# Attention stages ahead of weight splits, and transposes later in TensorE's queue

## The chip, the cores and the metric

The kernel runs on one core of one Trainium2 chip. The metric is the device time of one execution in microseconds. The kernel was run three times: median 1540.57, from 1539.96 to 1541.12. One more execution was taken with the hardware profiler; all rows below come from it.

## The reference

Two blocks run one after the other on a sequence of 256 tokens of width 1024, in float32, each with its own two layers of weights (DEPTH = 2).

The first block's layer is a hybrid mixer, a cross attention and a gated feed-forward, each followed by a layer norm of a scaled residual sum:

```
mix = hybrid_mixer(h, ...)                    # RG-LRU branch and sliding-window attention, gated, projected
h = layer_norm(DEEPNORM_ALPHA * h + mix, ln1_g[l], ln1_b[l])
h = layer_norm(DEEPNORM_ALPHA * h + cross_attention(h, mem, ...), ln2_g[l], ln2_b[l])
h = layer_norm(DEEPNORM_ALPHA * h + swiglu(h, ffn_wi[l], ffn_wo[l]), ln3_g[l], ln3_b[l])
```

The sliding-window attention has 16 query heads and 2 key heads of width 64, rotary positions on the first 16 columns of a head, a window of 128 keys and a sink in the softmax. The second block's layer is differential attention (4 heads, each the difference of two softmaxes, with a relative bias) beside a Hyena branch (three short convolutions and two long convolutions through the Fourier transform), gated, projected and added to the input after an RMS norm:

```
h = rms_norm(x, pre_norm[l], NORM_EPS)
w = p[:, :, 0] - lam * p[:, :, 1]             # differential attention's weights
z = fft_long_conv(hv, filt[:, 0], flt_bias[l, 0]) * hx1
z = fft_long_conv(z, filt[:, 1], flt_bias[l, 1]) * hx2
x = x + rms_norm(m @ w_out[l], post_norm[l], NORM_EPS)
```

## The kernel before, in words

Every large matrix product is made of three matmuls: each operand is split into a high part of reduced precision (fp32r) and the rest, and high x high, high x low and low x high are summed in PSUM. Weights come from memory in chunks of 1 MB (three raw buffers, tag raw). `split_one` (from line 213) splits a chunk in two halves: ScalarE writes the high part wh (L229), VectorE the rest wl (L231), into four pairs of buffers, so that splits can run up to four halves ahead of the matmuls. `run_stream` goes through the chunks in order: before each half it lets due stages run (`pump`), issues the half's matmuls, and then the split of the half that is four further on. A half is 24 matmuls of 256 columns (`fm`, weights stationary) or 12 of 512 columns (`tm`, activations stationary), and `pump` is called once more in its middle.

Everything that is no chunk is written as a generator (a stage list) that is kept in a list with a due time: `ln_co` transposes a normed block of 128 tokens, `swa_co` rotates queries and keys, transposes them (kt, qt) and spawns two `swa_run` (one a key head), which make scores (sc), a softmax, transposes of the probabilities (pt) and the product with the values (y); `cross_co` does cross attention; `diff_co` does differential attention for one block of tokens (scores ds, transposes dw, product o); `hyena_co` the long convolutions (dft, c). Each `yield` gives the time until the next stage is due. The planner's clock `self.t` counts TensorE work alone: n/2.4 ns for a matmul of n columns (four times that for float32), 107 for a transpose. So the due times in the table `L` set how much TensorE work stands ahead of a stage in TensorE's queue, and TensorE (and the DMA queue of SP) run in just that written order (`MAN`).

ScalarE, VectorE and GpSimd are not in `MAN`: their order is made by the scheduler, which takes instructions by their place in the written program. `advance` runs a stage inside `high_priority(offset=co.pri)`, with `pri` from the table `PRI` by the generator's name: its instructions count as if written that many places earlier. Cross attention has had 60 there, the filters' transforms -60.

In a norm, `ln_evac` makes block 0 of the tokens first (L568, L571 write t), then block 1; `ln_co` yields `ln_0` (500), transposes block 0, yields `ln01` to `ln12` less `ln_0`, and transposes block 1 (tiles tx; ScalarE and VectorE split them, L350 and L351). Behind the last norm of the first block's cross attention no chunk stands, and the planner fills with filter pieces (fh). `rope` (5000) is the due time between the rotation on VectorE and the transposes of rotated keys (kd) and queries. PSUM has two pools of four tiles: one for `fm` products, one for all stages and `tm`.

Of the kernel before, what the change touches and what calls it, by code (L numbers as in the profile page):

```python
# [40 lines left out]
NSLOT = 29  # L41
NTMP = 8
NKEEP = 5
PRI = {'filter_dft': -60, 'cross_co': 60, 'filter_end': 30, 'rnn_co': 30, 'mlp_co': 60}

L = dict(
    vec=6000, flt=12000, fh=1200, fe=18000, prep=15000, mlp=7500, sc=11000, rnn=7000, rnn2=11700,
    pt=3000, tx=0, spec=6000, sp0=3000, sp1=5000, sp2=5000, sp3=5000, ds=9000, dn=8960, do=5500,
    z=12000, cn=1000, cp=2000, ln_0=500, ln01=3500, ln02=5500, ln03=6000, ln11=5000, ln12=4000, pre0=5100,
    pre1=5000, rope=5000, sw0=1120, sw_end=1500, sw1=1000, sw2=1500, cv0=800, cv1=1050, rnn3=1800,  # L50
    rnn_end=3000, cx0=1500, cx1=1000, cx2=800, cx_end=1500, ml=7200, fm=3000, fe0=4000, eo0=6000,
    eo1=12000, eo2=8000, fd=6000, di0=1500, dw=850, di_end=1500, c30=770, c31=1300, hy0=1300,
    hy1=2000, hy2=500, hy3=1600, hy_end=2000, pre_n=3000, pre_n1=2300, prep2=30000, mem=10200)
# [50 lines left out]
class Net:  # L104
# [26 lines left out]
    def spawn(self, gen, bg=False):  # L131
        co = Co(gen, self.t, PRI.get(gen.__name__, 0))
        (self.bg if bg else self.chains).append(co)
        return co
# [1645 lines left out]
```

## Time and profile before

| what | value |
|---|---|
| median of 3 runs | 1540.57 us |
| the profiled execution | 1539.61 us |
| its span, first to last instruction | 1537.7 us |
| TensorE busy (PE) | 1500.0 us, 98% |
| weight loads (PEld) | 1387.4 us, 90% |
| VectorE (DVE) | 1095.2 us, 71% |
| ScalarE (ACT) | 862.1 us, 56% |
| GpSimd (POOL) | 83.7 us, 5% |
| mean granted TensorE clock | 0.992 |

Matmuls are pipelined: one of 256 columns is shown with some 283 ns, but the next starts 120 ns behind it. So a gap in TensorE's queue is read from the starts, or from the wait that the timeline puts in brackets behind a row.

### The profile page before, as it was taken

To read this page: it belongs to the slowest core of one execution; us is meant where nothing else is said; L and a number is where in the kernel's file an instruction comes from. 1 tells how busy PE (TensorE), PEld (TensorE's weight loads), DVE (VectorE), ACT (ScalarE), POOL (GpSimd) and SP (SyncE) were. 2 spreads that over 40 slices of the span, in tenths; PEclk is the share of its full clock that TensorE was granted. 3 is DMA by queue.
4 is the path that set the end of the run, shared out by engine and by line. 5 is a ranking of instruction groups with operands and counts; after the bars stand their busy time and mean duration, and the time that the engine had idled before them with its cause. 6 is when DMAs were issued, how large, how long until landed. Compare 5 with 4: busy or idle time off the path is not lost. (4 is left out here: it accounts for less than half of the span.)

```text
span 1537.7 us, 25746 instructions
## 1 busy us (share of the span) xinstructions
PE 1500.0 (98%) x10588; PEld 1387.4 (90%) x10588; DVE 1095.2 (71%) x1590; ACT 862.1 (56%) x1338; POOL 83.7 (5%) x152
## 2 busy tenths in 40 slices
PE   8999999999999999999999999999999999999997
PEld 6889999989999989899989798999798998898996
DVE  5876767668665477858676776555897987797865
ACT  5789444545444445797445556644545755555742
POOL 4001000000000000001010010000000010000000
PEclk9999999999999999999999999999999999999998
DMA  8435655445545545436555476565355356354542
GB/s 284 139 111 165 219 182 175 170 160 196 188 165 191 191 165 165 138 119 224 192 190 194 151 245 195 166 240 191 98 160 178 118 166 216 112 170 137 162 157 80
DMA packets 202982, 263.93 MB, mean 172 GB/s; under 512 B 5491, under 2 KB 163413, under 8 KB 202864
## 3 DMA queue, kind: packets, MB, share of 16 engines
q1 hardware_dynamic: 197232, 246.43, 48.5%
q0 software_dynamic: 5632, 15.86, 3.6%
q8 instruction: 83, 1.36, 0.4%
q14 instruction: 35, 0.29, 0.1%
HBM read 261.21 MB, written 2.11 MB: 171 GB/s over the span
## 5 line engine op out<-in xcount | busy, mean ns | idle before, releaser
L231 DVE TENSOR_TENSOR wl<-raw,wh 128x1024 fp32r<-128x1024 f32 x464 | 567.1, 1226 | 294.6 <-ACT wh L229 292.6
L229 ACT ACTIVATE wh<-raw 128x1024 fp32r<-128x1024 f32 (+1 forms) x465 | 490.2, 1057 | 443.2 <-PE fm L361 247.7
L361 PE MATMUL fm<-n2h,wh 128*128 128x256 f32 x640 | 176.6, 286 | 1.2 <-ACT n2h L350 1.2
L361 PE MATMUL fm<-n2l,wh 128*128 128x256 f32 x640 | 174.7, 283 | 0.0
L361 PE MATMUL fm<-n2h,wl 128*128 128x256 f32 x640 | 174.5, 283 | 0.0
L361 PE MATMUL fm<-h2h,wh 128*128 128x256 f32 x704 | 171.4, 284 | 0.0
L361 PE MATMUL fm<-h2h,wl 128*128 128x256 f32 x704 | 170.8, 283 | 0.0
L361 PE MATMUL fm<-h2l,wh 128*128 128x256 f32 x704 | 170.7, 283 | 0.0
L361 PEld LDWEIGHTS fm<-h2h,wh 128*128 128x128 f32 x704 | 124.0, 192 | 3.6 <-issue 1.9
L361 PEld LDWEIGHTS fm<-n2h,wh 128*128 128x128 f32 x640 | 119.9, 192 | 3.3 <-ACT n2h L350 1.7
L361 PEld LDWEIGHTS fm<-h2h,wl 128*128 128x128 f32 x704 | 122.7, 192 | 0.1
L361 PEld LDWEIGHTS fm<-h2l,wh 128*128 128x128 f32 x704 | 122.7, 192 | 0.0
L361 PEld LDWEIGHTS fm<-n2l,wh 128*128 128x128 f32 x640 | 119.8, 192 | 0.4 <-DVE n2l L351 0.4
L361 PEld LDWEIGHTS fm<-n2h,wl 128*128 128x128 f32 x640 | 119.8, 192 | 0.2
L361 PE MATMUL fm<-h3h,wh 128*128 128x256 f32 x256 | 71.2, 288 | 0.0
L361 PE MATMUL fm<-xTh,wh 128*128 128x256 f32 x256 | 70.9, 287 | 0.0
L361 PE MATMUL fm<-h3h,wl 128*128 128x256 f32 x256 | 70.1, 284 | 0.0
L361 PE MATMUL fm<-h3l,wh 128*128 128x256 f32 x256 | 70.0, 284 | 0.0
L361 PE MATMUL fm<-xTh,wl 128*128 128x256 f32 x256 | 69.8, 283 | 0.0
L361 PE MATMUL fm<-xTl,wh 128*128 128x256 f32 x256 | 69.8, 283 | 0.0
L361 PE MATMUL ff<-wh,ah 128*128 128x512 f32 x176 | 68.9, 392 | 0.0
L361 PE MATMUL ff<-wl,ah 128*128 128x512 f32 x176 | 68.7, 390 | 0.0
(433 smaller groups left out, 3650.1 us busy)
## 6 DMA issues: line engine op xcount, KB each, us to landing
raw<-in_w_in_dram SPq DMA_DIRECT2D x89, 1024.0 KB, 5.2
raw<-in_ffn_wi_dram SPq DMA_DIRECT2D x44, 1024.0 KB, 5.0
raw<-in_ffn_wo_dram SPq DMA_DIRECT2D x22, 1024.0 KB, 4.8
raw<-in_w_out_dram SPq DMA_DIRECT2D x16, 1024.0 KB, 5.0
raw<-in_ckv_w_dram SPq DMA_DIRECT2D x16, 1024.0 KB, 5.4
raw<-in_w_br_attn_dram SPq DMA_DIRECT2D x8, 1024.0 KB, 5.0
raw<-in_w_br_rnn_dram SPq DMA_DIRECT2D x8, 1024.0 KB, 5.0
raw<-in_cq_w_dram SPq DMA_DIRECT2D x8, 1024.0 KB, 4.9
```

The source lines that it names most:

```text
L229: hi_ins = self.nc.scalar.activation(hi[:, i:i + q], s[:, i:i + q], AF.Copy)
L231: lo_ins = self.nc.vector.tensor_tensor(lo, s, hi.bitcast(F32), op=ALU.subtract)
L361: self.nc.tensor.matmul(out, lhsT=l, rhs=r, start=start, stop=stop)
```

## The change

Two entries are added to `PRI`: the stages of `swa_run` and of `diff_co` now count as written 60 places earlier. In `L`, `ln_0` goes from 500 to 2200 and `rope` from 5000 to 6400. No instruction is added or taken away.

```diff
-PRI = {'filter_dft': -60, 'cross_co': 60, 'filter_end': 30, 'rnn_co': 30, 'mlp_co': 60}
+PRI = {'filter_dft': -60, 'cross_co': 60, 'filter_end': 30, 'rnn_co': 30, 'mlp_co': 60,
+       'swa_run': 60, 'diff_co': 60}
 
 L = dict(
...
-    z=12000, cn=1000, cp=2000, ln_0=500, ln01=3500, ln02=5500, ln03=6000, ln11=5000, ln12=4000, pre0=5100,
-    pre1=5000, rope=5000, sw0=1120, sw_end=1500, sw1=1000, sw2=1500, cv0=800, cv1=1050, rnn3=1800,
+    z=12000, cn=1000, cp=2000, ln_0=2200, ln01=3500, ln02=5500, ln03=6000, ln11=5000, ln12=4000, pre0=5100,
+    pre1=5000, rope=6400, sw0=1120, sw_end=1500, sw1=1000, sw2=1500, cv0=800, cv1=1050, rnn3=1800,
```

## Rows read from the trace of the kernel before

**Rows 1.** The page: busy time by engine, granted clock in 40 slices, ScalarE's splits.
```profile
PE 1500.0 (98%) x10588; PEld 1387.4 (90%) x10588; DVE 1095.2 (71%) x1590; ACT 862.1 (56%) x1338; POOL 83.7 (5%) x152
...
PEclk9999999999999999999999999999999999999998
...
L229 ACT ACTIVATE wh<-raw 128x1024 fp32r<-128x1024 f32 (+1 forms) x465 | 490.2, 1057 | 443.2 <-PE fm L361 247.7
```

**Rows 2.** TensorE's waits: who waited for whom, us in total, times, longest.
```profile
PE tx L373 <- DVE t L571: 6.0, 4, 3.0
...
PE pt L373 <- ACT scs L669: 1.9, 1, 1.9
...
PE kt L373 <- DVE kd L610: 1.2, 1, 1.2
...
PE ds L361 <- DVE dsc L1432: 0.9, 2, 0.4
PE c L361 <- ACT wT L1464: 0.7, 2, 0.4
```

**Rows 3.** The chain that ended last: start, us, engine and line, count.
```profile
1135.17 2.87 PE fm L361 x24
```

**Rows 4.** TensorE's timeline, layer 0: start, us, instruction, count [idle before, releaser].
```profile
50.58 0.27 PE L373 MATMUL kt<-ident,kd 128*128 128x128 f32 x1
52.06 0.55 PE L373 MATMUL kt<-ident,kd 128*128 128x128 f32 x3 [1.20 <-DVE kd L610]
```

**Rows 5.** TensorE's timeline, sliding-window attention of layer 1.
```profile
626.83 1.13 PE L361 MATMUL sc<-kv,qT 64*128 64x256 f32 x8
...
642.43 2.17 PE L373 MATMUL pt<-ident,scs 128*128 128x128 f32 x8 [1.90 <-ACT scs L669]
```

**Rows 6.** VectorE's timeline in the same stretch.
```profile
636.85 1.28 DVE L658 SCALAR_TENSOR_TENSOR scs<-sc,mask 128x512 f32<-128x512 f32 x2
...
639.24 1.22 DVE L231 TENSOR_TENSOR wl<-raw,wh 128x1024 fp32r<-128x1024 f32 x1
...
640.44 1.22 DVE L231 TENSOR_TENSOR wl<-raw,wh 128x1024 fp32r<-128x1024 f32 x1
```

**Rows 7.** A window behind it: busy us (count) by engine, granted clock, DMA share, GB/s.
```profile
642.40:646.00 3.60, 3.57 (x16) 2.96 (x17) 0.38 (x3) 3.60 (x11) 0.00 (x0) 0.53 0.77 265
```

**Rows 8.** TensorE's timeline, differential attention of the second block's layer 0.
```profile
1217.44 1.13 PE L361 MATMUL ds<-qk,qk 64*128 64x256 f32 x6 [0.44 <-DVE dsc L1432]
1218.93 0.50 PE L361 MATMUL c<-Yh,dft 128*128 128x512 f32 x1 [0.36 <-ACT wT L1464]
```

**Rows 9.** VectorE's timeline in the same stretch.
```profile
1215.51 1.27 DVE L1378 TENSOR_TENSOR t<-AB 128x512 f32<-128x512 f32 x2
1216.71 0.67 DVE L1432 SCALAR_TENSOR_TENSOR dsc<-ds,bias 128x512 f32<-128x512 f32 x1
```

**Rows 10.** TensorE's timeline, norms behind feed-forward (layer 0) and cross attention (layer 1).
```profile
556.39 1.32 PE L373 MATMUL tx<-ident,t 128*128 128x128 f32 x8 [1.40 <-DVE t L571]
...
564.75 1.03 PE L373 MATMUL tx<-ident,t 128*128 128x128 f32 x8
...
884.72 1.93 PE L373 MATMUL tx<-ident,t 128*128 128x128 f32 x8 [3.04 <-DVE t L571]
```

**Rows 11.** VectorE's timeline in the same two stretches.
```profile
561.83 1.41 DVE L571 SCALAR_TENSOR_TENSOR t<-t,rs,gb 128x512 f32<-128x512 f32 x2
...
881.28 0.67 DVE L351 TENSOR_TENSOR h2l<-tx,h2h 128x512 fp32r<-128x512 f32 x1
```

**Rows 12.** VectorE's timeline in cross attention of layer 0.
```profile
292.85 1.22 DVE L231 TENSOR_TENSOR wl<-raw,wh 128x1024 fp32r<-128x1024 f32 x1
293.98 0.16 DVE L930 TENSOR_SCALAR cst<-cst 128x2 f32<-128x2 f32 x1
```

**Rows 13.** ScalarE's timeline at the gates of layer 1.
```profile
669.51 1.28 ACT L752 ACT_TABLE_LOAD   x1
```

**Rows 14.** A window over the gates of layer 1, columns as in rows 7.
```profile
664.00:690.00 26.00, 26.00 (x211) 24.04 (x210) 14.56 (x20) 25.17 (x57) 0.88 (x1) 1.00 0.51 163
```

## The prediction

> **What bounds the kernel now.** I read the page's first parts, then the waits of TensorE alone, then the timelines where one of its waits touches an attention or a norm. TensorE is busy for 98% of the span at full granted clock [rows 1]; no matmul is added or removed, so the change can only alter the gaps in TensorE's queue. Its whole queue order is written by the planner; ScalarE and VectorE get theirs from the scheduler. The gaps that the edited lines can reach are few [rows 2]: the norms' transposes 6.0 us in 4 waits, the probabilities' transposes 1.9 in one, the rotated keys' 1.2 in one, differential attention 0.9 and 0.7 in two each: 10.7 us of idle time in all. That, and what a lowered clock costs after a long gap, is the ceiling. The reader should see in the PE timelines that each gap names a VectorE or ScalarE instruction, and in the VectorE timelines what stood ahead of that instruction.
>
> The planner's clock decides places. A matmul of 256 columns is 256/2.4 = 106.7 ns on it, and it looks for due stages every 12 matmuls, 1280 ns. On the chip 24 matmuls take 2.87 us [rows 3], so one such step is 1.44 us of cover.
>
> **Rotated keys (rope 5000 to 6400).** In layer 0 the first kt transpose runs at 50.58, the second at 52.06 [rows 4]: 1.48 apart, where the three from there on take 0.55 together, so some 1.35 is lost to kd. 5000 falls due at the fourth step (5120). 6400 is five steps exactly, and the planner sums in floating point: starting from the planner's time at which the stage is spawned, 29666.000000000036, my sum at the fifth step is 36066.0 against a due time of 36066.00000000004, a hair early, so I expect the sixth step: 24 matmuls later. Either way (1.44 or 2.87) it is covered. Value: 1.4, bounds 1.2 to 1.5. Layer 1 has no gap here, so there the delay gains nothing; its whole chain of scores and transposes moves 2.9 later, and nothing asks for it before the output projections, 16 halves of 24 matmuls (46 us) after the gates. No DMA is issued by the moved transposes; SP's queue keeps its order.
>
> **Sliding-window stages ahead by 60.** The gap is in layer 1: the pt transposes wait 1.90 for exponentials [rows 5]. Their scores had left TensorE at 626.83 + 1.13 = 627.96, yet VectorE first touches them at 636.85, 8.9 later, and inside the chain two weight splits of 1.2 stand between the maxima and the negated maxima [rows 6]. VectorE was working off convolutions and splits in that time. Sixty places are about two and a half halves of 24 matmuls (7.2 us) of age, so the mask and maximum should go roughly 5 earlier even if the fills remain. Only the 1.90 is needed. After the gap the granted clock is 0.53 over 3.60 us [rows 7], a loss of 0.47 x 3.60 = 1.7. The Trainium skill, page "TensorE: Matmul & The Clock Gate", Part 1, says that the slow level is the default and that activity releases it; the trace agrees with 0.53 right behind this gap. By that rule a removed gap returns its 1.7 too, and a gap that is only halved may return nothing of it. Both ends: 0 (the fills decide, below) and 3.6; I take 3.3, because the chain moves by more than twice what is missing, less 0.3 for transposes that now meet the last of four exponentials.
>
> What pays is the splits. A split may start when its buffer is free, three halves (3 x 2.87 = 8.6) ahead of use, and takes 1.06 [rows 1] + 1.2; about 6.3 is in hand. One stage of scores is some 3 us of VectorE, and only splits younger than sixty instructions are overtaken, those needed last. I cost it at nothing; if a split already 4 us late were overtaken by a whole stage, TensorE would wait some 1 us, and that is in the range.
>
> **Differential attention ahead by 60.** In each layer of the second block the last scores wait for PSUM that L1432 has yet to read (0.44), then c waits for wT (0.36) [rows 8]; with the waits of both layers 1.6. L1432 runs at 1216.71, behind two L1378 of the Hyena chain [rows 9]. Going first it closes the gap, but then Hyena's Y pieces slip by up to three operations of 0.67 (2.0), and they feed the very c matmuls that come next; they finish about 2 before use now. What is late next is therefore c on Yl. Bounds: 1.6 gained, 1.5 lost; I take 0.8 gained, since c also starts on the older half of Y.
>
> **Norm transposes (ln_0 500 to 2200).** Block 0 of the tokens is due at the second step instead of the first. Block 1's due time is counted from there, so its step stays (worked through: fourth, fifth and fifth step for ln01, ln02, ln11, as before), but for ln03: before, 2136 + 5500 = 7636 misses the fifth look at 7256; now 3416 + 3800 = 7216 makes it. So at the end of layer 0's feed-forward block 0, which waited 1.40 [rows 10], gets 1.44 of cover, while block 1 moves from 564.75 to about 561.7; its data leave L571 at 561.83 + 0.7 = 562.5 [rows 11], a new wait of about 0.9. Net 0.5, bounds -0.2 and 1.4. At the end of layer 1's cross attention no weight chunk covers: two more filter pieces go ahead of block 0, and block 1 waits 3.04 for its data [rows 10]. There two h2l operations of block 0, 0.67 and as much again, stand between block 1's statistics and its normalization [rows 11]; later transposes make them unready, and the chain ends up to 1.3 earlier. I take 0.9, bounds 0 and 2.5 (with the clock given back). The first norm of layer 0 has the same form with one such operation, 0 to 0.6; I take 0.
>
> **Sum.** 1.4 + 3.3 + 0.8 + 0.5 + 0.9 = 6.9. The profiled execution took 1539.61 (span 1537.7 and 1.9 around it), 0.96 below the median 1540.57. 1539.6 - 6.9 = 1532.7, and 1533.7 on the scale of the median.
>
> **Rivals.**
> A, the priority does nothing where it matters. A scheduler that takes whatever is ready puts a split into the gap after each dependent operation. For it: cross attention has had its 60 all along, and still a split stands between its maximum and the scaled maximum [rows 12]. Against it: the 8.9 delay of the mask is no fill, there was always older work ready. Then only the moved transposes act: 1.4 + 0.5 + 0.9 = 2.8, or 1536.8, on the median's scale 1537.8.
>
> B, slower: table swaps in the gates. The keys' shift and the priority push exponentials between the gates' sigmoid and tanh. One swap is 1.28 [rows 13], and ScalarE has 26.00 - 25.17 = 0.83 to spare in that stretch [rows 14]. A split's lead there is partly spent; I take half of 6.3, 3.2. With n extra swaps a layer, TensorE loses n x 1.28 - 0.83 - 3.2; from four on that is a loss, from six a layer it outweighs the 6.9. With eight: 6.2 x 2 = 12.4, so 1532.7 + 12.4 = 1545.1, on the median's scale 1546.1. Against it: today the tail of the exponentials meets the gates with one swap, and the scheduler would have to alternate at each gate tile. The Trainium skill, page "ScalarE: Activation LUTs", section "Table sets: the hidden batching unit", warns of just this and gives about 2.7 us a switch in its examples; the trace has 1.28. By the page's figure four swaps a layer would do as much harm as eight; I hold to the row.
>
> C, trade in differential attention: c waits on Yl as long as is saved and layer 1's stage recovers only its gap, not the clock: keys 1.4, gap 1.9, a loss of 1.0 and the norms' 1.4 make 3.7, so 1535.9, on the median's scale 1536.9.
>
> **How the numbers follow.** Forecast 0.56, A 0.17, B 0.11, C 0.16. Predicted 1533.7. All gains at their upper bounds (1.5 + 3.6 + 1.6 + 1.4 + 2.5 + 0.6 = 11.2) give 1529.4, and other orders than I can see may add a little: low end 1528.5. The high end takes in A and C and the beginning of B: 1540.5. A measurement of this kernel can tell about 0.2% (3.1 us) from no change. Faster by that (below 1537.5): the forecast, C and a part of A, 0.74; the same: the rest of A and a mild B, 0.16; slower: 0.10.
>
> **What would show it.** Right: kt without a wait in layer 0; the pt wait of layer 1 gone and the clock at 1.00 over the 4 us behind it; ds and c waits below 0.8 in sum; the tx wait of the feed-forward's end moved from block 0 to block 1; the longest tx wait shorter than 3.04 by about 1. Wrong: pt still waiting with splits ahead of L665 (A), a new TensorE wait on wh or wl, more table loads on ScalarE between the gates (B), c waiting on Yl (C). New gaps in the filters' or first block's other stages would break the sum, since the whole order of two engines is drawn anew.

## The result, and the profile after

The changed kernel takes 1556.64 us (median of 4 runs, 1554.33 to 1558.92) against 1540.66 for the kernel before on the same chip (4 runs, 1539.96 to 1541.12): ratio 1.0111, 95% interval 1.0099 to 1.0123. It is 16 us slower; the forecast was 1533.7, 7 us faster, with a range that ended at 1540.5. The profiled execution of after took 1554.33, its span is 1552.4; it is the shortest of the four, so the traces of after and before lie 14.7 apart where the medians lie 16 apart.

The lines of the page that answer to [rows 1]. All line numbers of after are one higher, because the table of priorities takes two lines.

```profile
PE 1502.4 (97%) x10588; PEld 1388.0 (89%) x10588; DVE 1096.9 (71%) x1590; ACT 873.4 (56%) x1346; POOL 81.0 (5%) x152
...
L230 ACT ACTIVATE wh<-raw 128x1024 fp32r<-128x1024 f32 (+1 forms) x465 | 489.0, 1056 | 456.3 <-PE fm L362 265.1
```

The counts of TensorE, VectorE and POOL are those of before. ScalarE has eight instructions more, and the groups by line say which: 37 table loads where before had 29. Eight loads of 1.28 are 10.3 of the 11.3 us that ScalarE is busier. So before any stall is looked at, the page says that ScalarE now changes its function table eight times more. Four of the eight stand at the gates; the other four stand at the square roots of the recurrence (147.89 to 156.44 and 703.33 to 711.88).

TensorE's waits in after (who waited for whom, us in total, times, longest), beside [rows 2]:

```profile
PE tx L374 <- DVE t L572: 6.0, 4, 2.9
PE gate L362 <- ACT r L753: 5.4, 3, 2.0
PE c L362 <- ACT wT L1465: 3.8, 2, 1.9
...
PE tx L374 <- DVE h1l L352: 2.2, 1, 2.2
PE sc L362 <- ACT xch L351: 2.1, 2, 1.8
PE c L362 <- DVE Yl L352: 1.8, 4, 0.7
...
PE c L362 <- ACT Yh L351: 1.4, 2, 0.7
```

The waits of kt, pt and ds, which the change was to remove, are gone. In their place stand waits of the gates for their own sigmoids, of c for wT and both Y pieces, of the scores sc for xch (the high part of the gates' input, which ScalarE writes), and a second one of tx.

Where the time went is read by following one stream: the projections, gates and feed-forward matmuls of the main stream stand in the same order in all kernels here. Each number is the start of the same matmul in a kernel's trace minus its start in before, in us; the head gives the place by before's own clock, and a difference between two columns is what was lost (or gained) between the two places.

| kernel | 112, gates of layer 0 begin | 129, they end | 374 | 577 | 635 | 666, gates of layer 1 begin | 681, they end | 819 | 899 | 1197 | 1229, behind c | 1425 | 1451, behind c | end |
|---|---|---|---|---|---|---|---|---|---|---|---|---|---|---|
| after | -0.65 | 4.58 | 5.83 | 5.42 | 5.85 | 2.05 | 6.99 | 8.30 | 8.57 | 7.19 | 11.31 | 10.51 | 14.71 | 14.71 |
| e1, rope alone | 4.38 | 6.57 | 6.64 | 6.63 | 7.07 | 3.28 | 5.78 | 5.78 | 6.10 | 4.88 | 4.85 | 4.43 | 4.42 | 4.42 |
| e2, swa_run alone | 0.75 | 2.35 | 2.42 | 2.41 | 2.41 | 0.67 | 2.31 | 2.32 | 2.79 | 1.73 | 1.71 | 1.28 | 1.28 | 1.28 |
| e3, diff_co alone | 0.22 | 0.22 | 0.26 | 0.26 | 0.26 | 0.39 | 0.39 | 0.41 | 0.42 | 0.15 | 4.79 | 4.06 | 8.48 | 8.47 |
| e4, ln_0 alone | -0.57 | -0.57 | 0.53 | 0.12 | 0.12 | 0.76 | 0.76 | 3.42 | 2.42 | 0.45 | 0.42 | 0.71 | 0.71 | 0.70 |
| e8, two norms | -0.13 | -0.13 | -0.07 | -0.47 | -0.47 | 0.08 | 0.08 | 0.11 | -0.17 | -1.34 | -1.34 | -1.72 | -1.74 | -1.75 |
| e11, 6400, one table | 1.74 | 1.78 | 1.42 | 1.39 | 1.82 | -1.97 | -1.93 | -1.92 | -1.20 | -2.27 | -2.29 | -2.70 | -2.70 | -2.70 |
| e13, 6300, Gelu bound | 0.51 | 0.51 | 0.54 | 0.53 | 0.56 | -1.79 | -1.79 | -1.77 | -0.54 | -1.57 | -1.60 | -2.03 | -2.05 | -2.06 |
| e14, gains together | 0.34 | 0.34 | 0.36 | -0.04 | -0.01 | -3.30 | -3.30 | -3.30 | -3.67 | -4.89 | -4.86 | -5.11 | -5.13 | -5.13 |
| e16, splits held | 0.48 | 0.48 | -0.82 | 3.45 | 3.47 | 4.05 | 4.05 | 5.62 | 4.74 | 4.75 | 4.78 | 4.83 | 4.81 | 4.81 |
| e17, best | 0.59 | 0.59 | -1.20 | -1.61 | -1.58 | -4.90 | -4.90 | -4.88 | -5.78 | -5.79 | -5.81 | -5.79 | -5.74 | -5.75 |

After loses 5.2 and 4.9 in the two sets of gates, 4.1 and 4.2 at the two c, and 1 to 1.3 in each of two stretches of norms (129 to 374, 681 to 819); it gains 3.8 between 635 and 666, where the pt stall was. That gain is not the priority's alone: e1, which has only the later rope, gains the same 3.8 there, and e2, which has only the priority, 1.7. Losses that the forecast had priced at nothing, or at 1.5 at most, cover it.

One column is no effect of an edit. The 1.0 to 1.4 that after, e1, e2, e8, e11, e13 and e14 gain between 899 and 1197 (e4: 2.0) come at one place, 1097, nearly all of it, behind a wait of fd for ft that the edits leave as it was (3.1 in before, e8 and after). What differs is the clock there: the windows of before and of e8 (us, busy us and count of PE, PEld, DVE, ACT and POOL, granted clock, DMA share, GB/s):

```profile
1090.00:1100.00 10.00, 9.42 (x54) 8.20 (x53) 8.11 (x10) 4.95 (x9) 0.00 (x0) 0.85 0.34 105
1090.00:1100.00 10.00, 9.40 (x65) 8.40 (x64) 9.29 (x12) 5.91 (x10) 0.00 (x0) 0.98 0.33 105
```

TensorE is busy for as long in both, and the granted clock is 0.85 and 0.98. So two single traces can differ by a microsecond where the edit changed nothing, and steps below that are not read as effects here.

The gates of layer 0 on ScalarE in after (start, us, instruction):

```profile
113.52 1.28 ACT L753 ACT_TABLE_LOAD   x1
114.82 0.47 ACT L753 ACTIVATE r<-gate,v 128x256 f32<-128x256 f32 x1
115.31 1.28 ACT L670 ACT_TABLE_LOAD   x1
116.61 0.40 ACT L670 ACTIVATE scs<-scs,sst 128x128 f32<-128x128 f32 x1
...
120.39 1.28 ACT L753 ACT_TABLE_LOAD   x1
121.69 0.47 ACT L753 ACTIVATE r<-gate,v 128x256 f32<-128x256 f32 x1
```

And TensorE, in the same stretch (the last figure is the idle time before, with its releaser):

```profile
122.21 0.39 PE L362 MATMUL gate<-xch,wh 128*128 128x256 f32 x1 [2.04 <-ACT r L753]
```

The reader is to see the first sigmoid at 114.82 and the second at 121.69, 6.9 later: between them a load of the exponentials' table, the eight last exponentials of the second key head, and a load back. The gates' tiles of PSUM come from a pool of four; the second sigmoid empties the first of them, and TensorE stands until then. In layer 1 the same three loads stand at 668.92, 670.71 and 675.79, and a gate waits 2.04 at 677.61 and another 1.34 at 682.40.

### The profile page after: what moved, and what is told of

Read it like the earlier page. It is cut to its first block, busy times and chain, and to the rows that moved or that the text cites. A ratio compares the mean times of both kernels' runs of the same rounds, so it can differ in the third digit from the quotient of the medians.

```text
span 1552.4 us, 25739 instructions
## 1 busy us (share of the span) xinstructions
PE 1502.4 (97%) x10588; PEld 1388.0 (89%) x10588; DVE 1096.9 (71%) x1590; ACT 873.4 (56%) x1346; POOL 81.0 (5%) x152
```

## The experiments

### The four edits one by one

Each kernel is before with one edit:

```diff
e1: -rope=5000          e1: +rope=6400
e2: +PRI 'swa_run': 60
e3: +PRI 'diff_co': 60
e4: -ln_0=500           e4: +ln_0=2200
```

e1, expected: 

> The change's rope value alone (6400 for 5000), nothing else changed. In the trace of after, the stretch of the gates at about 116 to 131 us of layer 0 and its like in layer 1 cost about 5 us each against before, with three table loads on ScalarE where before had one: a sigmoid, then the second half's eight exponentials, then the sigmoids again. Theory 1 (the later rope is what brings the last exponentials behind the first sigmoid): both layers lose their 5 us here, the two waits at kt are saved in layer 0 (1.3), so 1540.6 + 10 - 1.3 = about 1549, and the extra table loads are in the trace. Rival (the priority of the sliding-window stages does it, by letting the exponentials overtake the sigmoids): no loss at the gates, 1540.6 - 1.4 = about 1539.

e2, expected: 

> The priority of the sliding-window stages alone (60), nothing else changed. Theory 1 (rope causes the loss at the gates): the wait of the pt transposes at 640 us of layer 1 (1.9, and the slow clock behind it) goes and nothing is lost at the gates, about 1540.6 - 3.5 = 1537. Rival (the priority causes it): 1540.6 + 10 - 3.5 = about 1547, with exponentials between the sigmoids of both layers.

e3, expected: 

> The priority of the differential-attention stages alone (60). After against before showed some 4 us lost in each layer of the second block where c waits for wT and for the two Y pieces. Theory (the priority lets the row maxima and the subtraction of diff pass the Hyena products on VectorE, so that Yh, Yl and with them wT come late): 1540.6 + 2 x 4 = about 1548.5. Rival (that loss needs the other edits, whose lag shifts the feed): within 1 us of 1540.6, and c waits no longer than the 0.4 of before.

e4, expected: 

> The later due time of the norm transposes alone (ln_0 2200 for 500). Theory (the later transposes free a slot on VectorE into which a whole weight split of 1.2 falls where before a residual of 0.67 did, so that the second block of transposes waits longer in layer 0's first norm and in layer 1's first, while the first block's wait in layer 0's feed-forward norm goes): 1540.6 + 1 to 3 = about 1542.5. Rival (the forecast's own terms hold, -0.5 and -0.9): about 1539.2.

Measured, against 1539.74 for before: e1 1544.59 (ratio 1.0038, 1.0024 to 1.0052), e2 1539.76 (1.0003, 0.9994 to 1.0013), e3 1547.25 (1.0049, 1.0032 to 1.0066), e4 1542.55 (1.0018, 1.0009 to 1.0028). By the medians 4.9 + 0.0 + 7.5 + 2.8 = 15.2 of the 16. That looks as if the losses added, but four intervals of 1.5 to 2.6 us either way leave some 4 us open, and by place they do not add: before the gates of layer 0 after is at -0.65 where e1 and e2 are at 4.4 and 0.8, and in the gates after loses more (5.2 and 4.9) than e1 and e2 together (3.8 and 4.1). None of the four edits gains on its own.

e1 bore out its theory in kind and not in place. The exponentials stand between the first and the second sigmoid there too, so it is the later rope that puts them there, not the priority:

```profile
119.13 0.47 ACT L752 ACTIVATE r<-gate,v 128x256 f32<-128x256 f32 x1
119.62 1.28 ACT L669 ACT_TABLE_LOAD   x1
120.92 0.40 ACT L669 ACTIVATE scs<-scs,sst 128x128 f32<-128x128 f32 x1
...
124.22 1.28 ACT L752 ACT_TABLE_LOAD   x1
125.52 0.47 ACT L752 ACTIVATE r<-gate,v 128x256 f32<-128x256 f32 x1
```

But the gates lose only 2.2 and 2.5; layer 0 loses 4.4 before them, most of it where pt waits 2.51 at 96.91 for exponentials that stand behind a second swap, a load, a Gelu and a load (92.59 to 96.24). The rest of the 10 that the theory expected did not come.

e2 is a loss and a gain that cancel. The pt transposes of layer 1 run without a wait, against [rows 5], and the clock is not lost behind them: 3.7 gained at 646. Half of it goes again a little later, where y waits for its own factors:

```profile
651.19 1.94 PE L361 MATMUL y<-pt,kv 128*64 128x512 f32 x8 [1.32 <-DVE rbs L699]
```

And at the gates ScalarE takes four later activations ahead of the second sigmoid:

```profile
119.69 0.47 ACT L752 ACTIVATE r<-gate,v 128x256 f32<-128x256 f32 x1
120.06 1.08 ACT L687 ACTIVATE pt<-pt 128x512 f32<-128x512 f32 x2
121.02 1.58 ACT L752 ACTIVATE ig<-gate,hb 128x256 f32<-128x256 f32 x4
122.44 2.05 ACT L752 ACTIVATE r<-gate,v 128x256 f32<-128x256 f32 x5
```

with a wait of 1.33 on TensorE at 121.92, and 1.6 lost by the stream at each of the two sets of gates. e2 also has the four loads at the square roots that after has, and its stream loses nothing there (2.35 at 129, 2.42 at 374). My theory counted only the gain, the rival only the table loads; neither had this.

### What the priority of the stages displaces

e5 sets the order at the gates right again:

```diff
+PRI 'swa_run': 60
-    s.last_gate = nc.scalar.activation(self.ch(g, c), ...)
+    with self.tc.high_priority(offset=120):
+        s.last_gate = nc.scalar.activation(self.ch(g, c), ...)
```

Expected: 

> The priority of the sliding-window stages (60) and, added to it, a priority of 120 for the gates' own activations. With the stages' priority alone the wait at the pt transposes of layer 1 went, and 1.4 and 1.5 us were lost in the two layers where a gate matmul waits for a tile of PSUM whose second sigmoid stands on ScalarE behind four tanh of later gates. Theory (the stages' priority gains its 3.4 and the order of the sigmoids takes it back): the sigmoids now stand in the order of their matmuls, no wait at the gates, 1539.7 - 3 = about 1536.7. Rival (whatever is put ahead on ScalarE, something else comes late, a weight split first of all): about 1540, with waits of TensorE for wh or wl.

Measured 1542.56 (1.0021, 1.0012 to 1.0030): the rival's mechanism, and dearer than its 1540. TensorE's waits of e5:

```profile
PE gate L361 <- ACT wh L229: 2.0, 2, 1.0
...
PE gate L361 <- DVE wl L231: 1.5, 2, 0.8
```

The sigmoids are in order and the weight splits of the gates' own weights are late instead. In both orders tried here something comes late; the priority chose which.

### The rope: a threshold, or the tables

e6 moves the rotated keys by one step of the planner instead of two:

```diff
-rope=5000
+rope=6300
```

Expected: 

> A rope of 6300 for 5000 and nothing else: by the planner's clock one step of 12 matmuls later, where 6400 came out two steps later. Theory (a threshold: the last exponentials fall behind the first sigmoid only from the second step on): both waits at kt in layer 0 gone, one table load before the sigmoids as in the kernel before, 1539.7 - 1.3 = about 1538.4. Rival (any delay of the chain costs in the same way): the gates lose again, 1543 or more.

Measured 1545.46 (1.0035, 1.0023 to 1.0046). The threshold that I had supposed is not there: the last exponentials come ahead of the first sigmoid, as the theory said, and the kernel loses as much. ScalarE, layer 0:

```profile
113.40 1.28 ACT L787 ACT_TABLE_LOAD   x1
114.69 1.06 ACT L787 ACTIVATE gr<-gr 128x1024 f32<-128x1024 f32 x1
115.77 1.28 ACT L669 ACT_TABLE_LOAD   x1
117.06 0.40 ACT L669 ACTIVATE scs<-scs,sst 128x128 f32<-128x128 f32 x1
```

and TensorE behind it:

```profile
117.61 3.18 PE L373 MATMUL pt<-ident,scs 128*128 128x128 f32 x8 [1.53 <-ACT scs L669]
```

Here it is the Gelu of the recurrent branch, work that nobody needs for many microseconds, that the scheduler put into a gap of ScalarE: 3.6 us with its two loads, just ahead of the exponentials that pt is waiting for. In before the same Gelu stands at 151.58, 37 us later. That gave a sharper theory, the tables, and three kernels for it. In e9 and e10 Tanh stands in place of that Gelu, in e11 also Exp in place of the gates' Sigmoid; the values of the replaced functions are left out.

```diff
e9, e10, e11: -AF.Gelu_apprx_tanh   +AF.Tanh
e10: -rope=5000   +rope=6300
e11: -rope=5000   +rope=6400   -AF.Sigmoid   +AF.Exp
```

e9, expected: 

> A control: the kernel before with Tanh in place of the Gelu of the recurrent branch (that function's values are left out), and nothing else. Tanh and Exp stand behind one table load in the trace of the kernel before, so this takes table loads away where exponentials and Gelu alternate. Both theories of the two kernels below expect 1538 to 1540 here, as the swaps were beside TensorE's work in the kernel before.

e10, expected: 

> The rope of 6300, with Tanh in place of the Gelu of the recurrent branch (its values are left out). The trace of rope 6300 alone showed, in each of the two layers, a table load, a Gelu and a table load (3.6 us) on ScalarE just ahead of the last eight exponentials, and TensorE waiting for them. Theory (the table swap is what the later chain ran into): without it the loss of 5.7 is gone and the 1.3 of the kt wait shows, 1.3 below the control with Tanh alone, about 1538. Rival (the later chain itself is too late, by its VectorE work and the order of its transposes): 4 or more above the control, about 1544.

e11, expected: 

> The change's rope of 6400, with every function near the gates taken from the exponentials' table: Exp in place of the gates' Sigmoid, Tanh in place of Gelu (the values of both are left out). Theory (table swaps around the last exponentials are the loss of 6 to 10 at rope 6400): no load between them, within 1.5 of the control with Tanh alone, about 1539. Rival (eight exponentials between two gates' activations hold the PSUM tiles by themselves, whatever the table): 4 or more above the control.

Measured, against 1539.60: e9 1538.38 (0.9992, 0.9983 to 1.0001), e10 1535.98 (0.9975, 0.9965 to 0.9985), e11 1536.62 (0.9979, 0.9970 to 0.9987). The same two values of rope that cost 5.7 and 4.9 with the tables mixed are 2.4 and 1.8 faster than the control once they are not. In e11 the eight exponentials still stand between the gates' activations. In layer 1 the order is that of e1: two activations of the gates, the exponentials, then the next gates. ScalarE there, in e1 and then in e11:

```profile
671.35 0.84 ACT L752 ACTIVATE r<-gate,v 128x256 f32<-128x256 f32 x2
672.21 1.28 ACT L669 ACT_TABLE_LOAD   x1
...
676.81 1.28 ACT L752 ACT_TABLE_LOAD   x1
```

```profile
664.32 0.86 ACT L752 ACTIVATE r<-gate,v 128x256 f32<-128x256 f32 x2
...
668.68 0.40 ACT L669 ACTIVATE scs<-scs,sst 128x128 f32<-128x128 f32 x1
...
669.16 0.83 ACT L752 ACTIVATE r<-gate,v 128x256 f32<-128x256 f32 x2
```

The stream loses 2.5 there in e1 and 0.04 in e11: here the exponentials alone cost nothing, the loads around them do. Layer 0 shows it less cleanly, since e11 has both first activations ahead of the exponentials where e1 has one. No run has rope 6400 with the functions intact and the swaps gone.

e13 does it with the functions intact, by a bound on the order (the code had such a bound already for the recurrence's exponentials):

```diff
-rope=5000
+rope=6300
+with self.tc.issue_after(s.last_gate.ins):
     for i in range(2): nc.scalar.activation(s.gr[i], s.gr[i], AF.Gelu_apprx_tanh)
```

Expected: 

> The rope of 6300 with the real Gelu, which may now only issue behind the last gate's activation; nothing is left out. Theory (the loss of rope 6300 is one pair of table loads with a Gelu between them, pulled ahead of the last exponentials because ScalarE had a gap there): the pair is gone, the waits at kt too, so the gain of the variant with Tanh (3.6 below the kernel before, of which 1.2 were the control's) comes with the function intact: about 1536.5. Rival (the Gelu now stands in the way later, ahead of the square roots of the recurrence): 1540 or more, with a wait at the branch's output projections.

Measured 1536.40 against 1539.41 (0.9982, 0.9974 to 0.9991). So a delay of the rotated keys does gain, as long as no foreign table comes between, though not where the forecast put it. In layer 0 the kt wait of 1.2 goes, and a wait of rb for pt (0.7) and one of y (0.2) come further down the same chain; the stream stands at 0.48 at 38 us and at 0.51 at 112. The gain is in layer 1, where pt waits 0.4 instead of 1.9 and the stream goes from 0.56 to -1.79 between 635 and 666.

The Trainium skill, page "ScalarE: Activation LUTs", section "Table sets: the hidden batching unit", says that functions are loaded in named sets, exp and tanh in one, gelu in another that is kept apart from the tanh-approximated Gelu used here, and that a kernel should batch by set. The traces agree that exp and tanh share one and this Gelu does not: with Tanh in place of Gelu the page of e9 has 23 loads instead of 29, and where one function stands makes 8.7 us: e6 is 5.7 above its kernel before, e13 is 3.0 below its own.

### Differential attention: what the priority passes

e7 raises the Hyena stages as well, e15 only their last one:

```diff
e7:  +PRI 'diff_co': 60, 'hyena_co': 60
e15: +PRI 'diff_co': 60
e15: +with self.tc.high_priority(offset=60): tt(t1[:, par, :], ...)
e15: +with self.tc.high_priority(offset=60): self.split(y[0][:, par, :], ...)
```

e7, expected: 

> Differential attention ahead by 60 and the Hyena stages ahead by 60 as well, so that their order among themselves is that of the kernel before and both pass weight splits. Theory (the 7.5 us of the priority alone come from passing the Hyena products, whose Y pieces the next matmuls read): c waits for wT and Y as in the kernel before, about 1540, within 1.5. Rival (they come from what is passed besides, splits and residuals): about 1547 again.

e15, expected: 

> Differential attention ahead by 60, and of the Hyena stages only the last one, sums, differences and splits of Y, ahead by 60 as well. Theory (Y alone is what c waited for; the other Hyena products need no place of their own): the waits of c go back to those of the kernel before, and fewer splits are passed than with the whole Hyena chain ahead, about 1541. Rival (two chains ahead of the splits are too many however they are chosen): 1543 or more, TensorE waiting for wl as it did with the whole chain ahead (6.1 in 4 waits).

Measured: e7 1544.03 (1.0024, 1.0015 to 1.0033), e15 1546.42 (1.0044, 1.0032 to 1.0056). In both, no matmul c waits any more. That alone would prove little, because TensorE now comes to c later, held up by splits; but the Y pieces are also ready earlier: the last Yl ends at 1225.4 in e3, at 1216.6 in e7 and at 1215.9 in e15 (1218.6 in before). So the priority of e3 made the Y pieces late by passing the Hyena operations. And in both the time is not back, because the splits are late now; this is e15:

```profile
PE fm L361 <- DVE wl L231: 6.3, 4, 2.4
```

Why each of the three orders (e3, e7, e15) lost is in a view of before, VectorE's windows around c, which starts at 1218.93 (us, busy us and count, granted clock, DMA share, GB/s):

```profile
1175.00:1185.00 10.00, 6.25 (x12) 1.00 0.60 199
1185.00:1195.00 10.00, 10.00 (x16) 1.00 0.37 117
1195.00:1205.00 10.00, 10.00 (x18) 1.00 0.19 58
1205.00:1215.00 10.00, 10.00 (x17) 1.00 0.47 152
1215.00:1225.00 10.00, 10.00 (x17) 1.00 0.42 134
```

VectorE is busy all through the 40 us from 1185 to 1225, and the order of before leaves waits of 0.44 and 0.36 [rows 8]. What goes ahead there delays something else. In after it was this, on VectorE:

```profile
1226.12 0.68 DVE L1433 SCALAR_TENSOR_TENSOR dsc<-ds,bias 128x512 f32<-128x512 f32 x1
1226.72 0.68 DVE L1379 TENSOR_TENSOR t<-AB 128x512 f32<-128x512 f32 x1
...
1227.91 0.68 DVE L1433 SCALAR_TENSOR_TENSOR dsc<-ds,bias 128x512 f32<-128x512 f32 x1
```

and on TensorE:

```profile
1226.45 0.50 PE L362 MATMUL c<-Yh,dft 128*128 128x512 f32 x1 [1.88 <-ACT wT L1465]
...
1228.11 0.50 PE L362 MATMUL c<-Yh,dft 128*128 128x512 f32 x1 [0.69 <-ACT Yh L351]
1229.31 0.80 PE L362 MATMUL c<-Yl,dft 128*128 128x512 f32 x1 [0.70 <-DVE Yl L352]
```

Against [rows 9] the mask L1433 and the Hyena operation L1379 have changed places. TensorE waits three times in 3 us, and its later c take up to 0.80 instead of 0.39: the clock is lost on top (window 1220 to 1230: granted clock 0.96, 1230 to 1240: 0.87).

### The norms: which two gain, and why three lose

e8 delays the transposes only in the two norms for which the forecast counted a gain. e16 delays all five, and holds the weight splits behind each norm's last operation on VectorE.

```diff
e8:  -yield L["ln_0"]
e8:  +yield (first := 2200 if (l, i) in ((0, 3), (1, 2)) else L["ln_0"])
e16: -ln_0=500   +ln_0=2200
e16: -nc.vector.scalar_tensor_tensor(x[:, s], x[:, s], rs, b[:, s], ...)
e16: +self.defer = nc.vector.scalar_tensor_tensor(x[:, s], x[:, s], rs, b[:, s], ...)
```

e8, expected: 

> The later due time of the norm transposes for two norms only, the last of layer 0 and the one after layer 1's cross attention, the two for which the forecast counted a gain; the other three keep 500. Theory (these two gain and the other three lose, two of them by a longer wait of the second block): about 1.5 less than the kernel before, 1538. Rival (the two gain nothing either, since TensorE's clock stays down longer behind the longer gap): 1540.

e16, expected: 

> The later norm transposes in all five norms, as in the change, and in addition the weight splits that come after a norm's statistics in program order may only issue on VectorE behind the norm's last operation. Theory (a split of 1.2 that fills the gap after the statistics is what the second block's transposes then wait for): the chain of each norm runs without a split inside, its waits fall, and the 2.8 lost by the due time alone come back and more, about 1538. Rival (the splits held back are late themselves): 1542 or more, with waits for wl right behind the norms.

e8 took 1537.72 (0.9983, 0.9974 to 0.9992): 2.0 below before. Not all of it is the two norms': in e8's trace they give 0.4 (end of layer 0) and 0.3 (behind layer 1's cross attention; 0.4 to 1.0 in e4, e12, e14, e16 and e17), and 1.2 is the clock near 1097. What was forecast of their waits happened: at the end of layer 0 block 0 waits no more and block 1 waits 0.6; behind the cross attention both h2l have left block 1's chain, whose longest wait only falls from 3.04 to 2.92, because TensorE also comes to it 0.6 earlier (881.06 instead of 881.68).

e4's median is 4.8 above that of e8. By the traces the other three norms lose 3.8: 0.5 at the first norm of layer 0, 0.6 behind its cross attention, 2.7 at the first norm of layer 1. In after, the first norm of layer 0 on VectorE shows the reason for the first:

```profile
251.00 0.20 DVE L563 BATCH_NORM_AGGREGATE mv<-bst 128x2 f32<-128x12 f32 x1
251.12 1.17 DVE L232 TENSOR_TENSOR wl<-raw,wh 128x1024 fp32r<-128x1024 f32 x1
252.21 0.14 DVE L460 TENSOR_SCALAR rs<-mv 128x1 f32<-128x1 f32 x1
```

Between the statistics and what is made of them the scheduler puts one ready operation. In before it was an h1l of 0.63, which the earlier transposes had made ready; with later transposes it is a split of 1.17: 0.54 longer, which is the 0.5 that the stream loses there. (Two more splits stand in that chain, in before too, at 243.41 and 245.15.) Behind the cross attention of layer 0 it is the same: in e4 a split of 1.17 at 353.69 where before has an h2l of 0.64, and a wait of tx of 0.53 that before does not have. At the first norm of layer 1 TensorE waits 2.15:

```profile
811.09 1.26 PE L374 MATMUL tx<-ident,t 128*128 128x128 f32 x8 [2.15 <-DVE h1l L352]
```

The filling split stands there as well, but the wait is another one. By the code the transposes do not read h1l; what they can want of it is the PSUM tile that it empties. In before block 0's residuals h1l run at 799.41 and 802.68, around block 1's normalization, and the wait is 0.54. With later transposes they are ready only when VectorE is in block 1's normalization, and run behind the whole of it, from 810.35.

e16 took 1540.68 (1.0017, 1.0006 to 1.0027), between theory and rival. Its profiled execution took 1544.68, 4.0 more, so the table's row and what follows hold for that execution and not for the median. The first norm gains (from 0.48 to -1.33 at 253, no wait of tx there at all): with all three splits held back its chain is shorter by 1.8, more than the 0.5 that the longer fill had cost. The last norm of layer 0 loses 4.3, since three held splits now run one behind the other only when the norm is done, and TensorE waits for the first of them:

```profile
561.26 3.49 DVE L231 TENSOR_TENSOR wl<-raw,wh 128x1024 fp32r<-128x1024 f32 x3
```

```profile
562.54 0.58 PE L361 MATMUL fm<-memTh,wl 128*128 128x256 f32 x1 [2.65 <-DVE wl L231]
```

### Versions that beat both kernels

e12 takes e8's two norms and the sliding-window priority for layer 1 alone, dropped before the gates. e14 adds e13. e17 adds to e14 the first norm of layer 0, with the splits held behind that norm only.

```diff
e12: +s.cos = cos = [self.spawn(self.swa_run(l, s, kv)) for kv in range(2)]
e12: +for c in cos: c.pri = 60 * l
e12: +    s.cos[kv].pri *= tb          (in swa_run, at each block of tokens)
e17: +if hold: self.defer = last       (hold: layer 0, first norm)
```

e12, expected: 

> A version meant to beat both kernels: the later norm transposes for the two norms that gain (alone 2.0 below the kernel before), and the priority of 60 for the sliding-window stages in layer 1 alone and only up to their first 256 keys' tiles, so that it is gone again before the gates. Theory (the 3.4 gained at the pt transposes of layer 1 and the 3.0 lost at the gates are separate): 1539.7 - 2.0 - 3 = about 1534.5. Rival (what passes the splits there has to be paid back at the gates all the same): about 1537.7, as without the priority.

e14, expected: 

> All that gained, in one kernel: rope 6300 with the Gelu behind the last gate, the two later norm transposes, and the priority of 60 for the first tiles of the sliding-window stages in layer 1. Theory (the gains lie in different stretches and add): 3.2 for the first, 2.0 for the second, 1.5 for the third, 1539.7 - 6.7 = about 1533. Rival (the first and the third move the same chain of layer 1, so only one of them counts there): about 1534.5.

e17, expected: 

> The version in which the gains were put together (rope 6300 with the Gelu behind the last gate, the two later norm transposes, the priority for the first tiles of layer 1), and in addition the first norm of layer 0 with the later transposes and the splits held behind its chain: that norm alone, because there the kernel with all five held was 1.9 ahead of the kernel before by its matmuls, while the norm at the end of layer 0 lost 5.6 to splits that came late. Theory (a filling split is what makes the later transposes of that norm costly): about 1533, no wait for wl behind that norm. Rival (the 1.9 is taken back in the cross attention that follows, as it was in part with all five): about 1535, as without it.

e12 took 1536.22 (0.9978, 0.9969 to 0.9987), 1.4 below e8 by the medians, each against its own before, where 3 were expected (the intervals overlap): the stream gains 1.8 between 635 and 666, not 3.4, as the y matmuls now wait 1.3 for L701. e14 took 1534.99 (0.9970, 0.9959 to 0.9981), nearer to the rival's 1534.5 than to 1533, though its interval takes in both. The traces decide: between 635 and 666 e14 gains 3.3, where e13 has 2.35 and e12 1.8, so the two parts act on the same chain of layer 1 and their gains overlap in part. e17 took 1533.95 against 1540.87 (0.9955, 0.9941 to 0.9968), 7 us or 0.45% faster than before and some 23 faster than the change. By the times alone it can't be told from e14. By the traces it gains 1.8 at its first norm, where TensorE waits no more: at that norm the splits in the chain are shown to be what made the transposes wait.

## Why the prediction was wrong, point by point

**Rotated keys, 1.4 gained.** The wait at kt went, and the transposes ran later, as said. Two steps failed. One is "nothing asks for it before the output projections": the exponentials of the delayed chain ask ScalarE for their table, between the gates' sigmoids or beside a Gelu. e1 puts the edit at 4.9 lost; e10, e11 and e13 show that the tables are the cause, and the swaps at the gates alone cost 2.2 and 2.5 in e1. The other is "the delay gains nothing" in layer 1: the gain is there (2.35 in e13, 3.8 in e1 and e11), and in layer 0 none is left, since the chain further down waits 0.9 of the 1.2 that kt no longer does.

**Sliding-window priority, 3.3 gained.** The gap and the clock behind it came back, 3.7 at pt in e2, but y then waits 1.3 further down the same chain, and 1.7 is left between 635 and 666. The mask started 6.9 us after its scores where before had 8.9: 2.0 earlier and not "roughly 5". The step that failed most is "I cost it at nothing", which weighed only the splits: e2 shows 1.6 lost in each set of gates, by sigmoids put behind later activations, e5 shows the splits paying when that is mended. All in all the priority alone changed nothing (1539.76 against 1539.74).

**Differential attention, 0.8 gained, bounds 1.6 and -1.5.** The mechanism of the lower bound was named, Y late for c; what failed is its size, a bound of 1.5 where 7.5 was measured (e3). I had the Y pieces finish 2 before use and let them slip by 2.0; I did not add that wT queues on ScalarE behind four exponentials that the priority also moves (1.88 of the wait), nor that the clock falls behind the gaps. What left no room for a slip is how full VectorE is: 10.00 of 10 in four windows.

**Norm transposes, 0.5 and 0.9 gained.** Right in kind for the two norms that were worked through: 0.5 and 0.9 forecast, 0.4 and 0.3 to 1.0 in the traces. That e8's time came out 2.0 lower is in part luck, the clock near 1097. The step that failed is "I take 0" for the first norm of layer 0 and no term at all for two others; an operation that leaves a gap was replaced by a longer one, and at the first norm of layer 1, the largest of the three, the residuals that empty PSUM came behind the other block's normalization. Together that cost 4.8 by the medians of e4 and e8, 3.8 by their traces.

**Rival B, chance 0.11,** was the right mechanism at the gates, with the wrong price. I let a swap cost its 1.28 against the slack of ScalarE over the whole stretch and against the splits' lead, and so needed four extra swaps a layer for any loss. Two cost 2.2 and 2.5 a layer in e1, where nothing else is changed; in after, with the priority too, the gates lost 5.2 and 4.9. Four more loads at the square roots cost nothing. What counts is not whether ScalarE has room for the loads but which instruction stands behind them: the second sigmoid holds a tile of PSUM, and TensorE's queue stops with it.

**As a whole,** the chance of 0.10 for slower came from cases each priced alone. The prediction said itself that the whole order of two engines is drawn anew, and then summed only over the places with a wait in before.

## What to carry to other kernels

Before work is put ahead of other work, ask for the windows of the engine that does both: where it is full, as ahead of c here, a priority only chose what would be late, and it cost more than the waits that it was to remove. Of an activation engine, list which function tables meet in the stretch, and bound the order of those that can wait; an order bound on one Gelu turned 5.7 lost (e6) into 3.0 gained (e13), while no priority on whole stages gained (e2, e3, e5, e7, e15). When an operation is made later, ask what the scheduler will put into the gap that it used to fill, and whether that is longer.

## What was not expected of the hardware

A table load cost ScalarE its 1.28 here and nothing else that can be seen: from the end of the first sigmoid (114.82 + 0.47) over one load to the first exponential at 116.61 it is 1.32. What it costs TensorE is another matter. In the window 117 to 131 of after TensorE is busy for 11.69 of 14.00 at a granted clock of 0.88, where before had 20.00 of 20.00 at 1.00 over 110 to 130: 2.3 of idle time, and 0.12 x 14 = 1.7 more for the clock. That is 4.0 of the 5.2 lost there; for the rest I have no row. At c three waits of 3.3 together, 2.5 more than the 0.8 of before, and the clock of the two windows above (0.04 x 10 + 0.13 x 10 = 1.7) make 4.2, where 4.1 was lost.

The clock did not come back alike behind like gaps: near 1097, behind the same wait, the granted clock of one window was 0.85 in before, 0.98 in e8 and 1.00 in e9.
